# Block steps for two groups' queries and keys, adding transfers for weight sums, and down sums tied to half turns

## The chip, the core and the metric

The kernel runs on one core of a Trainium2 chip. The time is that of one execution on the device, in microseconds (us). The engines are named as in the profile: PE is TensorE (matmuls), PEld its loading of weights, DVE VectorE, ACT ScalarE, POOL GpSimd, and SP the engine that starts most transfers. A transfer that adds to its destination is started from POOL's queue (q0 in the profile); SP's and ACT's transfers are plain ones (q1).

## What is computed

One decoder layer on 512 tokens of width 1024, in float32: a half-step SwiGLU feed-forward part, a token mixer, and a second half-step feed-forward part, each with a norm ahead and behind.

```python
h = rms_norm(x, ffn1_pre);  x = x + 0.5 * rms_norm(swiglu(h, w_gate, w_up, w_down), ffn1_post)
h = rms_norm(x, mix_pre);   x = x + rms_norm(token_mixer(h, w_in, ...), mix_post)
h = rms_norm(x, ffn2_pre);  x = x + 0.5 * rms_norm(swiglu(h, ...), ffn2_post)

def token_mixer(h, w_in, ...):
    proj = h @ w_in                   # queries, keys, values of both attentions, gates
    o_nsa = nsa_attention(...)        # first attention: compressed, selected and window branch
    o_dil = dilated_attention(...)    # second: 3 groups of 4 heads, dilation 1, 4, 16
    y = sigmoid(g_a) * (o_nsa @ w_nsa_o) + sigmoid(g_b) * (o_dil @ w_dil_o)
    return y @ w_mix_out
```

## The kernel before

**Precision.** Each float32 operand is split into a rounded part and a remainder: a cast on ACT (line 153) and a subtraction on DVE (line 154). A product is three matmuls (`mm3`, lines 176 to 178): high by high, high by low, low by high. A weight tile of 128 x 1024 numbers is split into the pair `whi`, `wlo`, of which there are three buffers.

**Block products.** The feed-forward parts, and in the second attention half of the merge gates, use a form of matrix product in which a 2 x 2 arrangement of quarter products takes seven in place of eight. The quarters of the activation (first or second half of the width, first or second 256 tokens) are `B11`, `B21`, `B22`, and four sums of them are `T1` to `T4`. The matching weights are quarters (P1, P2, P4) or sums of quarters (P5, P6, P3, P7). Each of the seven steps is 24 matmuls with 256 columns. The token sums are made on DVE by `mix_token_sums`, kept split in slots named `SP`, `V` and `x`.

**The second attention** (`dil`). Three groups of four heads; a *turn* is a pair of heads, (group, pair). `project` makes a turn's queries and keys: two weight splits, two projections of 24 matmuls with 512 columns, then `q_parts` and `k_parts`, which scale, permute and split the result from PSUM into the slots `Q`, `KA`, `KB` (6 ACT and 4 DVE instructions of 64 x 512; POOL zeroes half of each `KB` tile). `attend` does the scores and softmax of the turn's two heads: matmuls into an `S` bank, a bias and row minimum on DVE (line 942), an exponential with row sum on ACT (line 943). Between the turns stand the *block steps*: `unit_blocks` yields the seven steps of a lot of gates, of which there are two, and `STEPS` says how many steps follow each turn. Their weight sums are made on DVE from raw quarters in SBUF (lines 1395 to 1401, four of 128 x 1024 for each lot). After the last turn the softmax statistics of the second and third group go through memory to be brought into token order (`sdram`, lines 1506 and 1552), the groups' weights are computed, POOL scales the stored probabilities with them (line 1583), and PE transposes these (lines 1630 and 1643). In between PE makes the values.

**The first attention** (`nsa`) goes over 16 heads and branches. Behind each, `sums(m)` starts transfers on POOL's queue: `table_sums` makes the sums of the down weights for the last feed-forward part, in four sets of up to three of its eleven row pairs (`b` = 0, 3, 6, 9), eight transfers for a set: four plain copies between tensors in memory and four that add. A set starts every third head.

**Order.** A scheduler lays out each engine's instructions when the kernel is built, by the order of the program and what is ready; a block `issue_after(i)` keeps instructions behind `i` on its engine. On the chip each engine and each queue goes through its list in order, and waits where an operand isn't there.

Of the kernel before, what the change touches and what calls it, by code (L numbers as in the profile page):

```python
# [12 lines left out]
F32 = mybir.dt.float32  # L13
# [4 lines left out]
OP = mybir.AluOpType  # L18
# [14 lines left out]
AHEAD = 2  # L33
STAGED = 5
STEPS = (3, 3, 1, 4, 2, 1)
# [20 lines left out]
GROUPS += [[(C_VD, 256)], [(C_VD + 256, 512)]] + [[(C_GA + u * P, 2 * P)] for u in range(0, 16, 2)]  # L56
PLACES = {}
# [17 lines left out]
class Layer:  # L75
# [1262 lines left out]
    def mix_token_sums(self, names):  # L1338
# [6 lines left out]
        def less(dst, a, t):  # L1345
            nc.vector.tensor_sub(dst, part(self.xht, *a), t)
            nc.vector.tensor_add(dst, dst, part(self.xlt, *a))

# [13 lines left out]
        if "T2" in names:  # L1362
            self.t2 = new()
            less(self.t2, (4, hi), self.t1)
            keep("T2", self.t2)
# [6 lines left out]
        if "T4" in names:  # L1372
            less(self.t2, (4, lo), self.t2)
            keep("T4", self.t2)

    def unit_loads(self, u):

        b = {}
        for h in range(2):
            r = self.pool.tile([P, 2, 4, 256], F32, name="raw", tag="raw", bufs=3)  # L1380
            for f in range(2):
                b[h, f] = r[:, f]
                self.nc.sync.dma_start(r[:, f], self.columns((C_GA + (u + 2 * f) * P, 2 * P))[:, 4 * h:4 * h + 4])
        return b

    def unit_blocks(self, u, b):

        nc = self.nc
        st = {}
        st["P5"], st["P6"] = [self.sbt("tmp", [P, 4, 256], bufs=2) for _ in range(2)]  # L1390

        def prep(name):
            with self.tc.issue_after(self.last_fold):
                if name == "P5":
                    nc.vector.tensor_add(st["P5"], b[0, 1], b[1, 1])
                if name == "P6":
                    nc.vector.tensor_sub(st["P6"], st["P5"], b[0, 0])
                if name == "P3":
                    nc.vector.tensor_sub(b[1, 0], b[1, 0], st["P6"])
                if name == "P7":  # L1400
                    nc.vector.tensor_sub(b[0, 1], b[0, 0], b[0, 1])
            src = dict(P1=b[0, 0], P2=b[1, 0], P7=b[0, 1], P4=b[1, 1], P3=b[1, 0]).get(name)
            st["w" + name] = self.wsplit(st[name] if src is None else src, [4, 256])

        def run(name):
            hi, lo = st["w" + name]
            key, top = dict(P1=("X", "B11"), P2=("Y", "B21"), P6=("X", "T2"), P5=("Z", "T1"), P7=("X", "T3"), P4=("X", "T4"),
                            P3=("Y", "B22"))[name]
            start = name in ("P1", "P2", "P5", "P3")
            if start:  # L1410
                st[key] = self.bank(dict(X="T", Y="V", Z="T")[key])
            for n in range(2):
                c = slice(n * P, (n + 1) * P)
                for j in range(4):
                    self.mm3(st[key][:, n * 256:(n + 1) * 256], hi[:, j, c], lo[:, j, c], self.tops[top][0](j),
                             self.tops[top][1](j), start and n == 0 and j == 0, False, True)

        def store(f, half, v):
            n = u + 2 * f
            nc.sync.dma_start(self.gdram[n:n + 2, :, 256 * half:256 * half + 256].rearrange("n p c -> p n c"),  # L1420
                              v.rearrange("p (n c) -> p n c", n=2))

        def finish(name):
            if name in ("P1", "P6", "P7", "P4"):
                v = st[name + "c"] = self.slot("ring")
                nc.scalar.copy(v, st["X"])
            for key in dict(P2="Y", P7="Z", P6="Z", P3="Y").get(name, ""):
                v = st[dict(P2="P1c", P7="P7c", P6="P6c", P3="P6c")[name]]
                nc.vector.tensor_add(v, st[key], v)
            if name in ("P2", "P7", "P4", "P3"):  # L1430
                store(*dict(P2=(0, 0), P7=(1, 1), P4=(1, 0), P3=(0, 1))[name], v)

        for name in ("P1", "P2", "P5", "P6", "P3", "P7", "P4"):
            prep(name)
            run(name)
            finish(name)
            yield

    def dil(self, fillers, early_gates):
# [16 lines left out]
        def project(g, j):  # L1456
            if j == 0:
                bias[g] = []
                for n in range(2 if g == 0 else 1):
                    w = self.slot("W")  # L1460
                    width = 256 if g == 0 else P
                    for m in range(S // width):
                        sl = -slopes[4 * g + 2 * n + m] * (1, 4, 4)[g]
                        o = w[:, m * width:(m + 1) * width]
                        nc.vector.tensor_scalar(o, (base0, self.dm[:, 384:512], base2)[g], sl, None, op0=OP.mult)
                        bias[g].append(o)
                stats.append(self.sbt(f"dst{g}", [P, NT, 4, 2]))
                probs.append([])
            b, _ = self.proj_T(raws[g, j][:, :, 0:P])
# [4 lines left out]
        def attend(g, j, q, kb, ka):  # L1474
            st = stats[g]
            for half in range(2):
# [28 lines left out]
            if j == 1 and g:  # L1505
                nc.sync.dma_start(self.sdram[g - 1].rearrange("(n r) c -> n r c", r=4), st.rearrange("p t h s -> p t (h s)"))
# [4 lines left out]
        lots = []  # L1511

        def blocks(n):
            for _ in range(n):
                if next(lots[0], 0) == 0:
                    lots.pop(0)
                    next(lots[0])

        def lot(u):
            lots.append(self.unit_blocks(u, self.unit_loads(u)))  # L1520
# [5 lines left out]
        for n, t in enumerate(turns):  # L1526
            pairs[t] = project(*t)
            if n == 0:
                lot(8)
                self.mix_token_sums(("T1",))  # L1530
            if n == 1:
                load(1, 0)
            if n == 2:
                self.mix_token_sums(("T2",))
                self.mix_token_sums(("T4",))
                self.mix_token_sums(("T3",))
            if n:
                attend(*turns[n - 1], *pairs.pop(turns[n - 1]))
                blocks(STEPS[n - 1])
            if n == 1:  # L1540
                load(1, 1)
            if n == 3:
                load(2, 0)
                lot(12)
                load(2, 1)
        attend(*turns[-1], *pairs.pop(turns[-1]))
        blocks(STEPS[-1])

# [161 lines left out]
    def mixer(self, post, finish, sums):  # L1710
# [21 lines left out]
        self.nsa(fill_half, sums)  # L1732
# [34 lines left out]
        self.dil(pieces(), lambda: [gate(d, 0, "KB") for d in range(EARLY)])  # L1767
# [155 lines left out]
    def run(self, out):  # L1923
# [10 lines left out]
        def boundary(post, pre, store, tags=None, shift=0):  # L1934
# [3 lines left out]
            def finish(t, gain):  # L1938
# [3 lines left out]
                if pre is not None:  # L1942
# [8 lines left out]
                   lambda m: [self.table_sums(a["d2"], td[1], b, m - b) for b in range(0, NP, 3)])  # L1951
# [51 lines left out]
```

## Time and profile before

| | us |
|---|---|
| median of 3 runs | 1110.22 (1108.45 to 1110.34) |
| the profiled execution | 1110.36 |
| its span | 1108.5 |
| PE busy | 1090.5 |
| DVE busy | 908.0 |
| ACT busy | 652.3 |
| POOL busy | 229.3 |

Busy time of PE covers the whole of a matmul, while the next one has begun already; the pace of the matmuls is read from their starts in the timeline. The stages that matter here, from the timeline: the first attention's heads run until about 517 us, the second attention's projections, scores and block steps from there to about 632, its values, transposes and outputs follow. A releaser in the profile is what an engine waited for last.

### The profile page before, as it was taken

What the parts mean: (1) busy time and instruction counts of PE and PEld (TensorE: products, weight loads), DVE (VectorE), ACT (ScalarE), POOL (GpSimd) and SP (SyncE); (2) the same over time, 40 slices, a digit from 0 to 9 for tenths busy, and PEclk for the clock granted to TensorE, in tenths of its full rate; (3) what the DMA queues carried; (4) which work ended last, traced back from release to release, by engine and by line L of the source; (5) the groups of instructions that cost most, each with busy time, mean ns of one, the idle gap of its engine ahead of it and who ended that gap; (6) DMA issues with size and microseconds to landing.
All of it is one profiled execution on the core that took longest, in us unless ns stands there. A gap on an engine that the chain in (4) does not pass through costs nothing.

```text
span 1108.5 us, 18921 instructions
## 1 busy us (share of the span) xinstructions
PE 1090.5 (98%) x7022; PEld 977.3 (88%) x7022; DVE 908.0 (82%) x1547; ACT 652.3 (59%) x1166; POOL 229.3 (21%) x312
## 2 busy tenths in 40 slices
PE   9999999999999999999999999999999999999997
PEld 7899999988789887777889998877989999998886
DVE  6989999998787988787977547876878999989575
ACT  7455555567565778675667636744435555567452
POOL 0444454310020056463000085001000000000001
PEclk9999999999999999999999999999999999999999
DMA  9899999999863498995231623573334444468862
GB/s 343 258 292 325 295 279 292 296 331 331 296 214 115 146 276 245 276 257 122 87 133 59 208 63 120 201 263 111 107 110 138 135 136 124 141 220 297 282 184 103
DMA packets 82652, 227.55 MB, mean 205 GB/s; under 512 B 12513, under 2 KB 17665, under 8 KB 79617
## 3 DMA queue, kind: packets, MB, share of 16 engines
q1 hardware_dynamic: 66192, 174.18, 46.3%
q0 software_dynamic: 16224, 51.91, 18.6%
q8 instruction: 55, 0.90, 0.3%
q14 instruction: 37, 0.30, 0.1%
q10 hardware_dynamic: 144, 0.26, 0.1%
HBM read 191.66 MB, written 57.72 MB: 225 GB/s over the span
## 4 chain that ended last, share of the span: by engine, by line
PE 69%; DVE 12%; ACT 7%; DMA 5%; POOL 3%; issue 3%; SPq 0%; DVEq 0%; POOLq 0%; ACTq 0%
PE pb_F L177 8%; PE pb_F L178 7%; PE pb_F L176 7%; PE pb_S L178 6%; PE pb_S L177 6%; PE pb_S L176 6%; PE pb_T L178 5%; PE pb_T L176 5%; PE pb_T L177 5%; DVE wlo L154 3%; DMA SP_s<-odram 2%; PE pb_V L177 2%; PE pb_V L178 2%; PE pb_V L176 2%; ACT whi L153 2%
## 5 line engine op out<-in xcount | busy, mean ns | idle before, releaser
L154 DVE TENSOR_TENSOR wlo<-raw,whi 128x1024 fp32r<-128x1024 f32 (+2 forms) x212 | 250.2, 1185 | 100.7 <-ACT whi L153 98.6
L153 ACT CAST whi<-raw 128x1024 fp32r<-128x1024 f32 (+2 forms) x212 | 215.3, 1019 | 149.8 <-PE pb_F L177 39.5
L176 PE MATMUL pb_F<-xhl_t,whi 128*128 128x512 f32 (+1 forms) x368 | 126.5, 344 | 0.4 <-DVE xhl_t L254 0.2
L178 PE MATMUL pb_F<-xhl_t,wlo 128*128 128x512 f32 (+1 forms) x368 | 125.6, 341 | 0.0
L177 PE MATMUL pb_F<-xhl_t,whi 128*128 128x512 f32 (+1 forms) x368 | 125.4, 341 | 0.0
L197 POOL TENSOR_TENSOR rs_t<-rs_t,mhalf_t 128x1 f32<-128x1 f32 x20 | 13.3, 666 | 465.4 <-DVE rs_t L193 465.4
L176 PE MATMUL pb_S<-xhl_t,whi 128*128 128x256 f32 (+1 forms) x280 | 83.3, 297 | 0.0
L177 PE MATMUL pb_S<-xhl_t,whi 128*128 128x256 f32 (+1 forms) x280 | 83.1, 297 | 0.0
L178 PE MATMUL pb_S<-xhl_t,wlo 128*128 128x256 f32 (+1 forms) x280 | 83.1, 297 | 0.0
L176 PEld LDWEIGHTS pb_F<-xhl_t,whi 128*128 128x128 f32 x368 | 69.2, 188 | 8.2 <-DVE xhl_t L254 0.9
L178 PEld LDWEIGHTS pb_F<-xhl_t,wlo 128*128 128x128 f32 x368 | 69.2, 188 | 7.5 <-DVE wlo L154 0.5
L177 PEld LDWEIGHTS pb_F<-xhl_t,whi 128*128 128x128 f32 x368 | 69.2, 188 | 6.8 <-issue 0.2
L153 ACT CAST whi<-tmp_t 128x1024 fp32r<-128x1024 f32 x40 | 40.6, 1051 | 37.0 <-DVE tmp_t L529 23.5
L1184 POOL TENSOR_SCALAR SP_s<-SP_s,st_t 128x384 f32<-128x384 f32 (+2 forms) x48 | 51.9, 1225 | 47.7 <-DVE st_t L1120 20.5
L177 PE MATMUL pb_T<-xhl_t,whi 128*128 128x256 f32 x216 | 59.9, 277 | 0.0
L176 PE MATMUL pb_T<-xhl_t,whi 128*128 128x256 f32 x216 | 59.9, 277 | 0.0
L178 PE MATMUL pb_T<-xhl_t,wlo 128*128 128x256 f32 x216 | 59.8, 277 | 0.0
L177 PEld LDWEIGHTS pb_S<-xhl_t,whi 128*128 128x128 f32 x280 | 52.6, 188 | 2.2
L176 PEld LDWEIGHTS pb_S<-xhl_t,whi 128*128 128x128 f32 x280 | 52.6, 188 | 2.2
L178 PEld LDWEIGHTS pb_S<-xhl_t,wlo 128*128 128x128 f32 x280 | 52.6, 188 | 2.2
L154 DVE TENSOR_TENSOR wlo<-tmp_t,whi 128x1024 fp32r<-128x1024 f32 x40 | 48.7, 1217 | 2.2 <-ACT whi L153 2.0
L176 PE MATMUL pb_T<-SP_s,whi 128*128 128x256 f32 x176 | 48.9, 278 | 0.0
(894 smaller groups left out, 3551.9 us busy)
## 6 DMA issues: line engine op xcount, KB each, us to landing
raw<-in_gu_dram SPq DMA_DIRECT2D x64, 512.0 KB, 4.8
raw<-tdram SPq DMA_DIRECT2D x40, 512.0 KB, 5.2
PT_s<-in_d_dram POOLq DMA_DIRECT2D x66, 256.0 KB, 6.7
raw<-in_d_dram SPq DMA_DIRECT2D x30, 512.0 KB, 4.5
raw<-in_w_in_dram SPq DMA_DIRECT2D x15, 1024.0 KB, 5.0
tdram<-in_d_dram POOLq DMA_DIRECT2D x18, 768.0 KB, 10.0
tdram<-PT_s POOLq DMA_DIRECT2D x44, 256.0 KB, 5.5
CP_s<-in_gu_dram SPq DMA_DIRECT2D x20, 512.0 KB, 4.2
```

The lines of the kernel that those rows point to most:

```text
L153: self.last_cast = self.nc.scalar.copy(dsthi, src).ins
L154: self.last_sub = self.nc.vector.tensor_sub(dstlo, src, dsthi.bitcast(F32)).ins
L176: mm(out, lhi, rhi, start=start, stop=False, skip_group_check=skip)
L177: mm(out, lhi, rlo, start=False, stop=False, skip_group_check=skip)
L178: self.last_mm = mm(out, llo, rhi, start=False, stop=stop, skip_group_check=skip).ins
L197: nc.gpsimd.tensor_tensor(out=r, in0=v, in1=self.mhalf, op=OP.pow)
L1184: self.last_pool = nc.gpsimd.tensor_scalar(pp, pp, st[:, 1, t:t + 1], None, op0=OP.mult).ins
```

## The change

- The queries and keys of groups 1 and 2 are no longer projected turn by turn. Each group's 512 columns are a lot of seven block steps, like the gates. The order of lots is group 1, first gates, group 2, second gates: 28 steps in all. `project` for these groups makes only biases and statistics.
- The joined results of a lot go through `token_rows`, which makes scaled, permuted and split queries and keys for 256 tokens at a time, two steps after the result.
- The weight sums P5, P6, P3 and P7 are made in memory: `lot_sums` starts plain and adding transfers on POOL's queue during the first attention, eight for each pair of lots, 1 MB each. A step's weight (or sum) is loaded whole, two at a time, and split two steps ahead.
- All four token sums are made behind the first turn's projection. `T2` and `T4` have the opposite sign, and so have the sums that use them.
- The turns are taken by halves: after each head's scores and softmax, `PLAN` says how many steps follow. Of the down sums of the last part, the first set stays in the first attention; the other three are started behind the half turns, each behind a POOL copy that waits for that half turn's statistics.
- The statistics' store is started from ACT's queue.

The core of the diff (loop heads and new helpers in part):

```diff
-STEPS = (3, 3, 1, 4, 2, 1)
+PLAN = (1, 2, 2, 5, 2, 2, 3, 5, 2, 1, 2, 1)
+LOTS = (0, 2, 1, 3)
+BLOCKS = ("P1", "P2", "P6", "P5", "P7", "P3", "P4")
...
+    def lot_sums(self, m, step):
+        put = self.nc.gpsimd.dma_start
+        s1, s2, s4, s3 = [v[:, 2 * m:2 * m + 2] for v in self.ldram]
...
+        if step == 0:
+            put(s1, part(1, 0))
+            put(s3, part(0, 0))
+        elif step == 1:
+            put(s2, part(0, 0))
+            put(s4, part(0, 1))
+        elif step == 3:
+            add(s1, part(1, 1))
+            add(s3, part(1, 0))
+        elif step == 6:
+            add(s2, s1)
+        elif step == 9:
+            add(s4, s2)
...
+    def load_blocks(self):
+        r = self.raw_tile([2, D])
+        for i in range(2):
+            self.nc.sync.dma_start(r[:, i], self.block_at(len(self.ready)))
+            self.ready.append(r[:, i].rearrange("p (k f) -> p k f", k=4))
...
+    def block_split(self, n):
+        while len(self.splits) <= min(n + SPLITS_AHEAD, 7 * len(LOTS) - 1):
+            m = len(self.splits)
+            self.splits.append(self.wsplit(self.ready[m], [4, 256]))
+            if m % 2 and len(self.ready) < 7 * len(LOTS):
+                self.load_blocks()
...
+            if name in ("P1", "P6"):
+                v = st[name] = place()
+                nc.scalar.copy(flat(v), src["X"])
+            elif name == "P5":
+                v = st["P6"]
+                nc.vector.tensor_sub(flat(v), flat(v), src["Z"])
+            elif name in ("P2", "P3"):
+                v = st["P1" if name == "P2" else "P6"]
+                nc.vector.tensor_add(flat(v), src["Y"], flat(v))
+                result(0, name == "P3", v, 1.0)
+            elif name == "P7":
+                v = place()
+                nc.scalar.mul(flat(v), src["X"], -1.0)
+                nc.vector.tensor_add(flat(v), src["Z"], flat(v))
+                result(1, 1, v, 1.0)
+            elif name == "P4":
+                result(1, 0, st["X"], -1.0)
...
+                for i in range(2):
+                    nc.scalar.mul(sel(q[i], rows[i]), qs[rows[i]], 0.125 * sign)
+                for i in range(2):
+                    nc.scalar.mul(sel(kz[i], rows[i]), ks[rows[i]], sign)
+                    nc.scalar.mul(sel(ka[i], rows[1 - i]), ks[rows[i]], sign)
...
+            return lambda *v: late.append((done[0] + 1 + 1, lambda: result(*v)))
...
-                nc.sync.dma_start(self.sdram[g - 1].rearrange("(n r) c -> n r c", r=4), st.rearrange("p t h s -> p t (h s)"))
+                nc.scalar.dma_start(self.sdram[g - 1].rearrange("(n r) c -> n r c", r=4), st.rearrange("p t h s -> p t (h s)"))
...
+        self.load_blocks()
+        for j in range(2):
+            pairs[0, j] = project(0, j)
+            self.load_blocks()
+            if j == 0:
+                for name in ("T1", "T2", "T4", "T3"):
+                    self.mix_token_sums((name,))
+        for i, n in enumerate(PLAN):
+            (g, j), half = turns[i // 2], i % 2
+            if (j, half) == (0, 0) and g:
+                project(g, 0)
+            attend(g, j, half)
+            mark = self.sbt("mark", [P, 1])
+            with self.tc.issue_after(nc.gpsimd.tensor_copy(mark, stats[g][:, 0, 2 * j + half, 0:1]).ins):
+                sums(i)
+            blocks(n)
...
+        def early_sums(m):
+            self.lot_sums(0, m)
+            self.lot_sums(1, m - 5)
+            sums(0, m - 2)
+
+        def late_sums(m):
+            for i in range(1, 4):
+                sums(3 * i, m - (0, 3, 5)[i - 1])
...
-                   lambda m: [self.table_sums(a["d2"], td[1], b, m - b) for b in range(0, NP, 3)])
+                   lambda b, step: self.table_sums(a["d2"], td[1], b, step))
```

More of the change, by code (lines that the diff above doesn't have):

```diff
@@ L1372, in mix_token_sums @@
         if "T4" in names:
-            less(self.t2, (4, lo), self.t2)
+            nc.vector.scalar_tensor_tensor(self.t2, self.t2, -1.0, part(self.xht, 4, lo), op0=OP.mult, op1=OP.subtract)
+            nc.vector.tensor_sub(self.t2, self.t2, part(self.xlt, 4, lo))
             keep("T4", self.t2)
[L1376 to L1384, printed above, removed]
@@ L1386, in unit_blocks, with lot_pair @@
-    def unit_blocks(self, u, b):
-        nc = self.nc
[L1389 to L1408, printed above, removed]
+    def lot_pair(self, m, f, h):
+        o = PLACES[[seg for seg in PLACES if seg[0] == LOT_AT[2 * m]][0]][0]
+        return self.a["w_in"][:, o:o + 8 * D].rearrange("p (l f h c) -> p l f h c", l=2, f=2, h=2)[:, :, f, h]
@@ new lines, in block_split, with lot_blocks, order, flat @@
+    def block_split(self, n):
[4 more added lines that the diff above has]
+                self.load_blocks()
+        return self.splits[n]
+    def lot_blocks(self, at, result):
+        nc = self.nc
+        lot = LOTS[at // 7]
+        st, keys = {}, dict(P1=("X", "B11"), P2=("Y", "B21"), P6=("X", "T2"), P5=("Z", "T1"), P7=("X", "T3"), P4=("X", "T4"),
+                            P3=("Y", "B22"))
+        tags = dict(X="F", Y="V", Z="F") if lot < 2 else dict(X="T", Y="V", Z="T")
+        home = []
+        if lot < 2:
+            for t in [self.sbt("tmp", [P, 2, S], bufs=2) for _ in range(2)]:
+                home += [t[:, 0], t[:, 1]]
+        def order(b):
+            return b.rearrange("p (m n r) -> p m r n", m=2, r=4) if lot < 2 else b
+        def flat(v):
+            return v.rearrange("p (m r n) -> p m r n", m=2, r=4) if lot < 2 else v
+        def place():
+            return home.pop(0) if home else self.slot("ring")
+        for n, name in enumerate(BLOCKS):
+            hi, lo = self.block_split(at + n)
+            key, top = keys[name]
@@ L1418, in store @@
[L1418 to L1436, printed above, removed]
+                    self.mm3(st[key][:, m * 256:(m + 1) * 256], hi[:, j, c], lo[:, j, c], self.tops[top][0](j),
+                             self.tops[top][1](j), start and m == 0 and j == 0, False, True)
+            src = {k: order(b) for k, b in st.items() if k in "XYZ"}
+            if name in ("P1", "P6"):
[15 more added lines that the diff above has]
+                result(1, 0, st["X"], -1.0)
@@ L1475, in attend, with gate_rows, result @@
+        def gate_rows(u):
+            def result(f, half, v, sign):
+                if sign < 0:
+                    b, v = v, self.slot("ring")
+                    nc.scalar.mul(v, b, sign)
+                n = u + 2 * f
+                nc.sync.dma_start(self.gdram[n:n + 2, :, 256 * half:256 * half + 256].rearrange("n p c -> p n c"),
+                                  v.rearrange("p (n c) -> p n c", n=2))
+            return result
+        def attend(g, j, half):
             st = stats[g]
-            for half in range(2):
+            q, kb, ka = pairs[g, j]
+            if half == 1:
+                del pairs[g, j]
+            for half in (half,):
@@ L1525, in dil @@
         load(0, 1)
[L1526 to L1547, printed above, removed]
+        self.ready, self.splits = [], []
+        self.load_blocks()
[14 more added lines that the diff above has]
+            blocks(n)
         nat = [stats[0]]
@@ L1730, in fill_half @@
                 fill(1)()
-        self.nsa(fill_half, sums)
+        NP = NF // 2
+        self.ldram = [tc.dram_tile([P, 4, D], F32, name=f"ldram{i}") for i in range(4)]
+        def early_sums(m):
[5 more added lines that the diff above has]
+                sums(3 * i, m - (0, 3, 5)[i - 1])
+        self.nsa(fill_half, early_sums)
         wn, wd = a["w_nsa_o"], a["w_dil_o"]
@@ L1765, in pieces @@
                         yield
-        self.dil(pieces(), lambda: [gate(d, 0, "KB") for d in range(EARLY)])
+        self.dil(pieces(), lambda: [gate(d, 0, "KB") for d in range(EARLY)], late_sums)
         behind = self.last_exp, self.last_cast
```

66 lines of the change are left out of this document (48 added, 18 removed).

## The prediction

> **What bounds the kernel now.** I read the page first, for the busy shares and the chain that ended last; then the table of windows over the second attention, where nearly every edit lies; then the timelines of TensorE and VectorE there, the view of the DMA queues, and the waits.
>
> ```profile
> span 1108.5 us, 18921 instructions
> PE 1090.5 (98%) x7022; PEld 977.3 (88%) x7022; DVE 908.0 (82%) x1547; ACT 652.3 (59%) x1166; POOL 229.3 (21%) x312
> PE 69%; DVE 12%; ACT 7%; DMA 5%; POOL 3%; issue 3%; SPq 0%; DVEq 0%; POOLq 0%; ACTq 0%
> ```
>
> ```profile
> 520.00:540.00 20.00, 19.39 (x93) 15.93 (x91) 19.76 (x26) 12.62 (x19) 0.52 (x1) 1.00 0.16 54
> 540.00:560.00 20.00, 20.00 (x126) 18.11 (x127) 19.58 (x35) 12.98 (x30) 0.52 (x1) 1.00 0.19 67
> 560.00:640.00 80.00, 79.95 (x545) 73.83 (x544) 51.09 (x129) 50.65 (x128) 3.12 (x6) 1.00 0.43 143
> 520.00:640.00 120.00, 119.34 (x760) 107.88 (x759) 90.44 (x189) 76.25 (x175) 4.17 (x8) 1.00 0.35 115
> ```
>
> The columns after the window are PE, PEld, DVE, ACT and POOL busy, the granted clock, the DMA share and GB/s. PE is full through the whole stage. Three things are seen beside it: DVE is full too from 520 to 560, POOL is almost idle (4 of 120 us), and the DMA engines are busy for a third (0.35). So a microsecond less of matmuls in this stage is a microsecond less of the kernel, as long as DVE, POOL and DMA, which the change loads, don't take PE's place.
>
> **What TensorE saves.** A busy PE hides the step between matmuls, so I take starts.
>
> ```profile
> 525.67 0.39 PE L177 MATMUL pb_F<-xhl_t,whi 128*128 128x512 f32 x1
> ...
> 531.34 0.39 PE L178 MATMUL pb_F<-xhl_t,wlo 128*128 128x512 f32 x1
> ...
> 537.34 0.28 PE L936 MATMUL pb_S<-KA_s,Q_s 128*128 128x256 f32 x1
> ...
> 542.87 0.28 PE L176 MATMUL pb_V<-xhl_t,whi 128*128 128x256 f32 x1
> ...
> 545.75 0.29 PE L176 MATMUL pb_T<-SP_s,whi 128*128 128x256 f32 x1
> ...
> 548.49 0.39 PE L176 MATMUL pb_F<-xhl_t,whi 128*128 128x512 f32 x1
> ...
> 629.71 0.27 PE L937 MATMUL pb_S<-KB_s,Q_s 128*128 128x128 f32 x1
> ```
>
> From 525.67 to 531.34 there are 25 steps of a 512-column matmul: 0.227 us each, so a projection of 24 takes 5.44 us. The two queries' and two keys' projections of a group take four: 21.8 us. In place of them stand seven blocks of 24 matmuls with 256 columns. A block whose moving operand is the activation itself takes 545.75 - 542.87 = 2.88 us, one with a sum kept in the SP slots 548.49 - 545.75 = 2.74 us. P1, P2 and P3 read the activation, and T3 lies in V and x slots, where I take the slower 2.88; P6, P5 and P4 take 2.74. Seven are 4 x 2.88 + 3 x 2.74 = 19.7 us. Each group saves 2.1 us, the two **4.1 us**. The 14 gate blocks, the scores (from 537.34, the last at 629.71) and the values are the same before and after.
>
> **What VectorE and ScalarE pay.** Here are the kinds of instruction that the edits add and remove.
>
> ```profile
> L154 DVE TENSOR_TENSOR wlo<-raw,whi 128x1024 fp32r<-128x1024 f32 x22 | 26.7, 1222 | 19.7 <-ACT whi L153 19.7
> ...
> L930 DVE SCALAR_TENSOR_TENSOR Q_s<-pb_F,Q_s 64x512 fp32r<-64x512 f32 x6 | 4.2, 694 | 0.1
> ...
> L1429 DVE TENSOR_TENSOR ring_s<-pb_T,ring_s 128x512 f32<-128x512 f32 x4 | 2.7, 685 | 0.9 <-ACT ring_s L1426 0.9
> L1395 DVE TENSOR_TENSOR tmp_t<-raw 128x1024 f32<-128x1024 f32 x2 | 2.4, 1222 | 2.1 <-DMA raw<-in_w_in_dram 2.1
> ...
> L1592 DVE TENSOR_TENSOR Q_s<-pb_F,Q_s 128x256 fp32r<-128x256 f32 x1 | 0.4, 416 | 0.0
> ```
>
> ```profile
> L153 ACT CAST whi<-raw 128x1024 fp32r<-128x1024 f32 x22 | 22.7, 1050 | 29.2 <-PE pb_F L177 25.1 <-PE pb_T L177 2.6 <-issue 1.2
> ...
> L1426 ACT COPY ring_s<-pb_T 128x512 f32<-128x512 f32 x8 | 4.7, 585 | 0.1
> ...
> L928 ACT ACTIVATE Q_s<-pb_F 64x512 fp32r<-64x512 f32 x6 | 3.6, 594 | 0.1
> ...
> L1591 ACT CAST Q_s<-pb_F 128x256 fp32r<-128x256 f32 x1 | 0.4, 368 | 0.0
> ```
>
> Splits go from 8 + 14 to 28: +6 x 1.22 on DVE, +6 x 1.05 on ACT. The eight weight sums of lines 1395 to 1401 leave DVE: -8 x 1.22. A pair's queries and keys took 6 ACT and 4 DVE instructions of 64x512; now each of two halves takes as many of 64x256. No row shows that shape; it lies between half of 0.69 (no gain or loss) and all of it (twice the cost). I take the 128x256 rows, 0.42 and 0.37, since duration goes by columns: DVE 32 x 0.42 - 16 x 0.69 = +2.4, ACT 48 x 0.37 - 24 x 0.59 = +3.6. Joining the products takes 16 DVE adds in place of 8 (+5.5) and 14 copies in place of 8 (+3.5). The sums: DVE +7.3 - 9.8 + 2.4 + 5.5 = **+5.4 us**, ACT 6.3 + 3.6 + 3.5 = **+13.4 us**. The last window holds 90.4 us of DVE and 76.3 of ACT in 120; with 96 and 90 in 116 neither is the bound on average, but the start is full already:
>
> ```profile
> 517.61 0.69 DVE L1217 TENSOR_TENSOR x_s<-pb_V,x_s 64x512 f32<-64x512 f32 x1 [1.66 <-ACT x_s L1216]
> ...
> 536.08 0.69 DVE L154 TENSOR_TENSOR SP_s<-CP_s,SP_s 128x512 fp32r<-128x512 f32 x1
> 536.69 1.22 DVE L1397 TENSOR_TENSOR tmp_t<-tmp_t,raw 128x1024 f32<-128x1024 f32 x1
> 537.83 1.22 DVE L1346 TENSOR_TENSOR CP_s<-xhl_t,CP_s 128x1024 f32<-128x1024 f32 x1
> ```
>
> From the last fold of the first attention (517.6 + 0.7 = 518.3 us) to the split that the tenth block needs, DVE has: the four token sums (10 passes at the 1.14 us between starts, 8 remainders at 0.61), 16.3; the first two pairs' parts and the second's splits (8 x 0.69 + 2 x 1.14), 7.8; ten block splits, 11.4; four half turns of softmax, four rows each at some 0.35, 5.5; joins, parts and biases of the first group, some 9. That is 50 us. PE is done with its projections at 537.34; four half turns of scores (about 0.95 each) and nine blocks are 29.4 us more, so it comes to the tenth block at 566.7: DVE has 48.4 us. Now the first 40 us of the stretch are as full (19.76 and 19.58 of 20) and cost PE almost nothing, because the token sums are spread past a second pair of projections, which the change takes out. Of a shortage of about 2 us I charge PE with **1.2 us**: zero if the joins of the last two blocks can wait, 2.4 if none can.
>
> **What DMA and the POOL queue pay.**
>
> ```profile
> q0 software_dynamic: 4608, 23.07, 64.6%
> q1 hardware_dynamic: 2581, 10.37, 21.0%
> ...
> raw<-in_w_in_dram SPq DMA_DIRECT2D x4, 1024.0 KB, 5.7
> raw<-in_w_in_dram SPq DMA_DIRECT2D x7, 512.0 KB, 9.1
> ...
> gdram<-ring_s SPq DMA_DIRECT2D x6, 256.0 KB, 7.5
> ```
>
> ```profile
> q1 hardware_dynamic: 6880, 13.72, 33.3%
> ...
> gdram<-ring_s SPq DMA_DIRECT2D x8, 256.0 KB, 2.3
> ```
>
> The first is the queues from 380 to 520 us (the first attention, which now carries all the down sums of the last part), the second from 520 to 645. The POOL transfers cost 0.646 x 140 / 23.07 = 3.9 us of all 16 engines per MB, SP's loads 0.21 x 140 / 10.37 = 2.8. The change swaps equal loads in the first attention: 16 transfers of 1 MB come, 24 of the 32 for the down sums go (16.8 MB either way), with only two after its eleventh head; I cost that at nothing. The 16.8 MB go to the second attention: 66 us of engines. Its weights grow as well, from 8.4 to 28 x 0.52 = 14.7 MB: +18 us on the 0.333 x 125 = 42 us of now. Together 126 us in a stage of about 120: **the DMA engines go from a third to full**. Who pays? Block weights are asked for about four blocks ahead, 11 to 15 us, and a load landed in 5.7 us (1 MB) or 9.1 (0.5 MB) beside the POOL transfers of the first attention; I charge nothing, the bound is a few microseconds in the two runs of five blocks. A late load would first hold its split, behind it on ACT and DVE the softmax rows and joins, and then PE.
>
> The POOL instructions that make adding transfers wait for earlier ones; behind them on POOL are the zeroing of key tiles, which comes free before the marks and has a whole turn to spare, and the scaling of the probabilities, which has none:
>
> ```profile
> 634.81 3.31 DMA sdram<-dst_t
> 638.19 1.82 DMA nat_t<-sdram
> ...
> 642.49 5.39 POOL PT_s L1583 x5
> ```
>
> ```profile
> 670.39 0.95 PE L1643 MATMUL pb_T<-ident_t,PT_s 128*128 128x128 f32 x7 [0.41 <-POOL CP_s L1583]
> ```
>
> In the chain, the last softmax statistics go through memory and back, POOL starts scaling at 642.5, and PE, with 40 us of other work after its last scores, arrives at the transposes 0.41 us too early, at 670.0. So any delay of that round trip is paid in full, as far as room isn't found. The change gives it some room: the last half turn's four rows stand alone after two blocks, where now eight rows run to 634.8, 5 us behind the scores at 629.7; half of them is about 2.4 us sooner. Against it stand two adding transfers, 1.3 MB or 5 us of engines, issued at that same half turn. I let the two cancel: **0 us**, bounds -0.4 (only the wait of now can go) and +8.0 (the rival below). Moving the statistics' store from SP's queue to ACT's costs one issue there and frees SP.
>
> The sum, on the profiled execution's own 1110.36 us (span 1108.5, 0.14 above the median): -4.1 + 1.2 + 0 = **-2.9 us, 1107.5**; against the median of 1110.22, 1107.3.
>
> **The rivals.**
>
> *The saving is eaten at the start.* DVE and ACT are in order, and PE has only two splits of lead (three weight buffers). For it: the two full windows, and the pair of projections that no longer covers the token sums. Against it: VectorE has 29 of 80 us free from 560 on. The whole shortage of 2.4 us, and 1 to 1.5 more in the runs of five blocks, where ACT has 15 us (5.3 of splits, 6.6 of parts, 3 of softmax and copies) to PE's 15: -4.1 + 2.4 + 1.3 = -0.4, **1109.8 us**. No measurable change; chance 0.25.
>
> *The statistics come home late.* The adds of the last turns wait for those two to three half turns earlier, and the DMA engines are full, so the transfers at the last half turn, and POOL behind them, slip; and the small store and load of the statistics share the engines with them. For it: a 256 KB store landed in 2.3 us on the quiet engines and in 7.5 beside the POOL transfers, 5.2 more; POOL has already waited for a transfer in this way, in the first attention, where PE's longest wait in all names VectorE:
>
> ```profile
> POOL tdram L1306 <- DMA tdram<-in_d_dram: 5.1, 1, 5.1
> ```
>
> ```profile
> PE pb_V L1208 <- DVE PT_s L154: 0.7, 2, 0.4
> ```
>
> Twice 5.2 on the round trip less 2.4 of room is +8.0. It decides from the point where the round trip, or POOL, is more than 2.4 us later than now. Against it: block loads end some 20 us before the end, which lets the engines catch up. With 8.0 and the -2.9 above: +5.1, **1115.3 us**; slower, chance 0.20. The Trainium skill, "DMA: Bandwidth & Descriptors", section "Queues, rings and completion order", says that a DMA engine serves its queue rows in turn and empties a whole packet from one before it switches. By that rule a store of many small rows waits behind one large packet at each turn, which speaks for this rival; the trace's 2.3 against 7.5 us agrees with it, but shows it only for rows of 2 KB.
>
> *The first attention gains too.* Only two POOL transfers are issued in its last five heads, where the wait of 5.1 us stands now. If 3 us of it reach PE today: -2.9 - 3 = -5.9, **1104.3 us**; chance 0.07. Against it: the 0.7 us above, and no PE wait there names POOL.
>
> **How the numbers follow.** The forecast has 0.48. A measurement of this kernel can tell about 0.2%, 2.2 us, from no change. Faster by more: 0.48 + 0.07 = 0.55; within: 0.25; slower by more: 0.20. The range reaches from 1103.8 (just below the third rival) to 1114.0: it takes in the first rival whole and the nearer half of the second's, and leaves out not quite 0.2.
>
> **What would show it.** TensorE should have 7 x 2 x 24 matmuls of 256 columns in place of 192 of 512, and the stage from 515 us to the last scores be about 3 us shorter. If VectorE is the cost, PE's waits between 550 and 570 us name the remainders of line 154 or the parts. If the statistics are, the wait ahead of the first transposes grows from 0.41 us, POOL's scaling starts more than 28 us before it, and the landing time of the statistics' store has grown from 3.3 us. Loads that land after their split is due would show as ACT's casts waiting for DMA. What would make me wrong altogether is a first attention that slows by its larger transfers (1 MB where now 768 KB), which I costed at nothing.

## The result, and the profile after

The changed kernel takes **1126.3 us** (median of 4 runs, 1125.4 to 1127.8) against 1110.3 us before in the same comparison: a ratio of 1.0149, with a 95% interval of 1.0131 to 1.0166. It is 16 us slower. The forecast was 1107.3 us and the range ended at 1114.0. The profiled execution took 1125.38 us.

The page of the changed kernel, span, busy time and the two large DMA queues:

```profile
span 1123.6 us, 19346 instructions
PE 1092.0 (97%) x7166; PEld 986.1 (88%) x7166; DVE 913.6 (81%) x1569; ACT 666.4 (59%) x1202; POOL 247.7 (22%) x340
...
q1 hardware_dynamic: 68208, 180.44, 47.0%
q0 software_dynamic: 20064, 68.69, 23.8%
```

TensorE's busy time grew by 1.5 us, DVE's by 5.6, and the engines that grew more are idle for much of the span: ACT by 14.1 us with 41% to spare, POOL by 18.4 with 78%. So the time looks like waiting, and the page can't say where. The table of windows over the second attention can (columns as before: PE, PEld, DVE, ACT, POOL, granted clock, DMA share, GB/s):

```profile
560.00:580.00 20.00, 18.64 (x159) 18.43 (x158) 16.68 (x39) 16.67 (x36) 3.88 (x9) 1.00 1.03 345
580.00:600.00 20.00, 20.00 (x172) 20.00 (x171) 13.64 (x38) 13.85 (x38) 6.20 (x12) 1.00 1.04 297
600.00:620.00 20.00, 12.17 (x80) 11.76 (x78) 3.23 (x5) 6.03 (x10) 1.67 (x2) 0.74 1.05 358
620.00:640.00 20.00, 14.98 (x111) 15.01 (x112) 15.87 (x37) 14.05 (x35) 2.84 (x5) 0.83 0.67 178
```

From 600 to 620 us every compute engine is slack at once: PE 12 of 20 us, DVE 3, ACT 6. Only the DMA share is full, at 1.05, and has been since 560 (a share of 1 or a little more is read as full here). TensorE's waits from 520 to 700 us, longest first (microseconds in total, times, longest):

```profile
PE pb_F L181 <- ACT tmp_t L1473: 6.7, 1, 6.7
PE pb_S L941 <- DVE KA_s L1542: 6.2, 1, 6.2
PE pb_T L181 <- ACT ring_s L1463: 1.4, 1, 1.4
```

Two waits make 12.9 us. The engines that they name are not to blame; their own rows say what they were waiting for. ScalarE's timeline in the stall (start, duration, and in brackets the idle time before it):

```profile
606.30 1.04 ACT L158 CAST whi<-raw 128x1024 fp32r<-128x1024 f32 x1 [6.99 <-DMA raw<-in_w_in_dram]
608.87 1.04 ACT L158 CAST whi<-raw 128x1024 fp32r<-128x1024 f32 x1 [1.52 <-DMA raw<-in_w_in_dram]
...
615.94 1.05 ACT L158 CAST whi<-raw 128x1024 fp32r<-128x1024 f32 x1 [5.53 <-DMA raw<-in_w_in_dram]
```

VectorE's timeline:

```profile
607.38 1.23 DVE L159 TENSOR_TENSOR wlo<-raw,whi 128x1024 fp32r<-128x1024 f32 x1 [8.52 <-ACT whi L158]
...
619.82 0.18 DVE L1638 TENSOR_TENSOR mn_t<-dst_t,nat_t 128x16 f32<-128x16 f32 x1 [8.05 <-DMA nat_t<-sdram]
619.91 0.68 DVE L1469 TENSOR_TENSOR tmp_t<-pb_V,tmp_t 128x512 f32<-128x512 f32 x1
```

ScalarE waits three times for a block weight, 14.0 us in all. VectorE waits behind it for the same weights, and then 8 us for group 1's statistics: the small minimum of line 1638 stands in its line ahead of the join of line 1469, and the key parts that PE wants come after that. The instructions of the block loads (line 1416) from 580 to 600 us show the source:

```profile
L1416 SPq DMA_DIRECT2D raw<-ldram x4: 320/380/2818, 579.7 to 597.4; - x4
...
L1416 SPq DMA_DIRECT2D raw<-in_w_in_dram x3: 328/346/423, 585.5 to 591.3; - x3
...
  ACT whi L158: 14.0, 3
...
DMA to landing us min/median/max: 8.7/20.9/25.4
```

The last line is the time from issue to landing: a load of 512 KB takes 20.9 us (median), 25.4 at most. By the prediction's count it is asked for 11 to 15 us ahead. In the trace of the kernel that has no sums in this stage (below), 10.4 to 19.2 us pass from the issue of a block load to the cast that needs it, for the loads issued from 560 to 605 us; this is called the lead. Late loads are the first suspect; the minimum on VectorE is a second, and the block steps themselves a third.

### The profile page after: what moved, and what is told of

The parts are those of the page before. It is cut to its first block, busy times and chain, and to the rows that moved or that the text cites. A ratio compares the mean times of both kernels' runs of the same rounds, so it can differ in the third digit from the quotient of the medians.

```text
span 1123.6 us, 19346 instructions
## 1 busy us (share of the span) xinstructions
PE 1092.0 (97%) x7166; PEld 986.1 (88%) x7166; DVE 913.6 (81%) x1569; ACT 666.4 (59%) x1202; POOL 247.7 (22%) x340
## 4 chain that ended last, share of the span: by engine, by line
PE 64%; DVE 15%; DMA 8%; ACT 7%; issue 3%; POOL 2%; SPq 0%; DVEq 0%; POOLq 0%; ACTq 0%
PE pb_S L183 7%; PE pb_S L182 7%; PE pb_S L181 6%; PE pb_F L183 6%; PE pb_F L182 6%; PE pb_F L181 6%; PE pb_T L183 4%; PE pb_T L181 4%; PE pb_T L182 4%; DVE wlo L159 4%; PE pb_V L181 2%; PE pb_V L182 2%; PE pb_V L183 2%; ACT whi L158 2%; DMA gdram<-ring_s 2%
## 5 line engine op out<-in xcount | busy, mean ns | idle before, releaser
L159 DVE TENSOR_TENSOR wlo<-raw,whi 128x1024 fp32r<-128x1024 f32 (+2 forms) x222 | 262.8, 1188 | 98.2 <-ACT whi L158 94.7
L158 ACT CAST whi<-raw 128x1024 fp32r<-128x1024 f32 (+2 forms) x222 | 226.1, 1020 | 139.5 <-PE pb_F L183 19.8
L202 POOL TENSOR_TENSOR rs_t<-rs_t,mhalf_t 128x1 f32<-128x1 f32 x20 | 13.3, 664 | 455.9 <-DVE rs_t L198 455.9
L181 PE MATMUL pb_F<-xhl_t,whi 128*128 128x256 f32 (+1 forms) x320 | 106.3, 332 | 0.4 <-DVE KA_s L926 0.2
L183 PE MATMUL pb_F<-xhl_t,wlo 128*128 128x256 f32 (+1 forms) x320 | 105.3, 329 | 0.0
L182 PE MATMUL pb_F<-xhl_t,whi 128*128 128x256 f32 (+1 forms) x320 | 105.0, 328 | 0.0
L181 PEld LDWEIGHTS pb_F<-xhl_t,whi 128*128 128x128 f32 x320 | 60.3, 188 | 5.8 <-issue 0.9
L183 PEld LDWEIGHTS pb_F<-xhl_t,wlo 128*128 128x128 f32 x320 | 60.2, 188 | 5.1 <-DVE wlo L159 0.5
L182 PEld LDWEIGHTS pb_F<-xhl_t,whi 128*128 128x128 f32 x320 | 60.3, 188 | 4.3 <-issue 0.2
L1189 POOL TENSOR_SCALAR SP_s<-SP_s,st_t 128x384 f32<-128x384 f32 (+2 forms) x48 | 49.0, 1051 | 50.5 <-DVE st_t L1125 20.2
L158 ACT CAST whi<-tmp_t 128x1024 fp32r<-128x1024 f32 x36 | 36.4, 1052 | 30.4 <-DVE tmp_t L534 23.5
L183 PE MATMUL pb_T<-SP_s,wlo 128*128 128x256 f32 x176 | 48.8, 277 | 0.0
```

The costliest lines, as they stand in the source:

```text
L158: self.last_cast = self.nc.scalar.copy(dsthi, src).ins
L159: self.last_sub = self.nc.vector.tensor_sub(dstlo, src, dsthi.bitcast(F32)).ins
L181: mm(out, lhi, rhi, start=start, stop=False, skip_group_check=skip)
L182: mm(out, lhi, rlo, start=False, stop=False, skip_group_check=skip)
L183: self.last_mm = mm(out, llo, rhi, start=False, stop=stop, skip_group_check=skip).ins
L202: nc.gpsimd.tensor_tensor(out=r, in0=v, in1=self.mhalf, op=OP.pow)
```

## The experiments

Theories at the start: **A**, full DMA engines make both the block weights and the statistics late, and both cost PE; **B**, only the order costs (VectorE's minimum ahead of the joins); **C**, late block weights alone; **D**, too much ScalarE and VectorE work in the runs of five blocks.

**Sums later, and the statistics moved.** Four kernels. The first issues the late sums after the last scaling on POOL:

```diff
-            mark = self.sbt("mark", [P, 1])
-            with self.tc.issue_after(nc.gpsimd.tensor_copy(mark, stats[g][:, 0, 2 * j + half, 0:1]).ins):
-                sums(i)
             blocks(n)
...
+        with self.tc.issue_after(scaled):
+            for i in range(len(PLAN)):
+                sums(i)
```

> All steps of the three late sets of down sums are issued after the last scaling on POOL, none at a half turn; everything else is as changed (1126.3 us). Theory A (16.8 MB of adding transfers fill the DMA engines at 560 to 620 us; block loads and group 1's statistics come late): the 16.2 + 3.8 us that PE loses between 600 and 640, and most of 3.2 + 2.5 us beside it, go: 1103 to 1107 us, ACT's casts wait under 1 us for loads. Rival B (the order alone: VectorE's minimum over group 1's statistics stands ahead of the joins and parts): a quiet round trip still costs some 4 us ahead of the joins, 1108 to 1112 us. Rival D (too much ACT and DVE work in runs of five blocks): the stall stays, 1120 us or more. If the transfers hurt the merge stage behind, that shows as new PE waits after 700 us.

The second leaves the sums and moves the statistics (the third kernel does both, the fourth has only the lines of `mn`):

```diff
+            with self.tc.issue_after(self.last_load):
                 nc.sync.dma_start(n_.rearrange("p t h s -> p t (h s)"), self.sdram[g].rearrange("(t p) c -> p t c", p=P))
...
+        with self.tc.issue_after(self.last_soft):
             nc.vector.tensor_tensor(mn, nat[0][:, :, :, 0], nat[1][:, :, :, 0], op=OP.min)
```

> The sums stay at the half turns; the two loads of statistics stand behind the last block load on SP's queue, and VectorE's first minimum behind the last softmax. Theory A: the wait of 6.2 us for DVE and what the lower clock adds to it go, the wait of 6.7 us for late loads stays: about 1116 to 1120 us. Rival B: both waits go, 1106 to 1110 us. Rival C (late loads alone; the minimum only waits in a gap that the loads make anyway): 1123 to 1126 us.

> Both edits. Theory A: within 2 us of the run with the sums later alone, 1102 to 1107 us, since a quiet round trip costs little. Rival B: 3 us or more below that run.

> Only VectorE's first minimum stands behind the last softmax; the loads of statistics stay where they are on SP's queue, ahead of two block loads. If VectorE's place in line is what the statistics cost, this is within 1 us of the run that moves both. If SP's queue is (a load of statistics that waits for its store holds block loads behind it), it stays near 1126 us and the other run is lower.

Measured: sums later **1144.2 us** (ratio 1.0314, 1.0299 to 1.0330), statistics behind **1125.9** (1.0146, 1.0129 to 1.0163), both 1142.4 (1.0297, 1.0281 to 1.0312), minimum alone 1127.4 (1.0162, 1.0146 to 1.0177). No theory had expected the first; its expectation named only the sign, new waits after 700 us. Its windows say why:

```profile
600.00:620.00 20.00, 19.29 (x164) 19.12 (x164) 15.37 (x31) 17.30 (x36) 0.00 (x0) 1.00 0.51 172
...
700.00:720.00 20.00, 11.34 (x51) 9.16 (x50) 7.94 (x17) 5.21 (x10) 3.94 (x7) 0.82 1.02 327
720.00:740.00 20.00, 14.82 (x50) 11.12 (x49) 8.07 (x13) 5.75 (x9) 3.33 (x4) 0.84 1.03 320
740.00:760.00 20.00, 4.06 (x9) 2.79 (x10) 5.93 (x9) 6.45 (x10) 2.45 (x3) 0.59 1.06 252
```

The second attention is whole again: PE 19.29 of 20 us where it had 12.17, at a DMA share of 0.51. The first transposes start at 668.9 us, 1.5 before those of the kernel before (670.39). But the same 16.8 MB, let loose at once, fill the engines from 685 to 770 us, and PE stalls there instead, by more. The stall has gone where the sums went: that rules out D, whose ACT and DVE work is all still in place.

Moving the statistics does what it says and buys nothing. TensorE's waits of that kernel:

```profile
PE pb_F L181 <- ACT tmp_t L1473: 7.2, 1, 7.2
PE pb_S L941 <- DVE KA_s L1542: 2.5, 1, 2.5
PE pb_S L181 <- ACT whi L158: 2.4, 1, 2.4
```

The wait for the key parts falls from 6.2 to 2.5 us and the last scores come 4.7 us sooner (640.1 against 644.8). But then PE waits for the value weights (the third row), and the first transposes start at 687.15 us, as in the changed kernel (687.04). So B falls as it stood: group 1's minimum is a wait in the shadow of others. A's price for this run, 1116 to 1120 us, was missed as well; 1125.9 us lies where C had put it. The run with the minimum alone can't be told from this one (their intervals overlap), nor the run with both edits from the one with the sums later. What holds the value weights is left open here and taken up by the last two runs.

**How many bytes it takes.** The sums are moved to where the engines are free: one step with each pair of the last part, some 17 us apart.

```diff
             if opened:
                 sums_behind(ev[:, 0:1], p + 1)
+            else:
+                mark = self.sbt("mark", [P, 1])
+                with self.tc.issue_after(nc.gpsimd.tensor_copy(mark, x[:, 0:1]).ins):
+                    for i in rest:
+                        self.table_sums(wd, td, 3 * i, p - (0, 0, 1)[i - 1])
```

`rest` is (1, 2, 3) with none left at the half turns, (2, 3) or (3,) with one or two sets left there. These and the fourth keep the statistics behind, so that they compare with 1125.9 us for all three sets. The fourth has all three at the half turns, with `accum_op` set to bypass: it leaves out the additions of these sets and moves the same bytes.

> As the run with the statistics behind, but the three late sets of down sums are issued one step at a time with the pairs of the last part (some 17 us apart, from 790 us on, where the DMA share is 0.3 to 0.5 without them). Theory C (the DMA engines are full at 560 to 620 us, block loads land later than they are asked ahead, nothing else): second attention as in the run with both edits, first transposes 2 us sooner than before; 66 us of engines spread over some 140 us of the last part give a share of 0.8 to 0.9 there, no new wait: 1107 to 1109 us. Rival (adding transfers on POOL's queue slow whatever runs beside them): new waits of PE in the last part, 1112 us or more.

> One of the three late sets stays at the half turns, two go to the last part. Theory C with a threshold: 22 us of engines more in the second attention leave the share under 0.9, block loads land in under 11 us, which is the least that they are asked ahead; within 1.5 us of the run with none at the half turns. Rival (each MB moved costs its share of the 18 us): 5 to 7 us above that run.

> Two of the late sets at the half turns, one in the last part. Threshold: 44 us of engines more, share near 1 in the run of five blocks at 590 to 605 us, loads land in 10 to 16 us: 2 to 8 us above the run with none. In proportion: 11 to 13 us above it.

> All three late sets at the half turns, with plain transfers of the same bytes in place of the adding ones: the additions of three of the four sets of down sums are left out. If it is the bytes that fill the engines: the stall stays, within 3 us of 1126 us. If adding is what is dear (its transfers hold an engine longer per byte): 1112 to 1120 us, with a DMA share at 560 to 620 well under 1.

The sets are not of one size: the first two that are left at the half turns have three row pairs each (6.3 MB), the third has two (4.2 MB). The shares are those of the windows, the landings those of the block loads issued from 580 to 600 us (median and longest):

| sets at the half turns | median us | ratio to before, 95% | DMA share 560:580, 580:600, 600:620 | landing us |
|---|---|---|---|---|
| 0 | 1107.9 | 0.9972 (0.9961 to 0.9983) | 0.54, 0.65, 0.51 | 4.4, 5.4 |
| 1 | 1108.0 | 0.9973 (0.9962 to 0.9985) | 0.88, 0.87, 0.63 | 5.8, 9.4 |
| 2 | 1113.7 | 1.0030 (1.0016 to 1.0043) | 1.03, 1.04, 0.79 | 14.7, 17.9 |
| 3 | 1125.9 | 1.0146 (1.0129 to 1.0163) | 1.03, 1.04, 1.04 | 23.2, 25.7 |
| 3, plain transfers | 1113.3 | 1.0022 (1.0012 to 1.0032) | 0.98, 1.00, 0.76 | 15.0, 18.7 |

This is a threshold, not a price by the byte. The first set, some 25 us of engines at the prediction's 3.9 us per MB, costs nothing (the landing stays under the lead), the second, of the same size, costs 5.7 us, and the third, the smallest, some 12. (The row of all three was measured in another comparison than the others; by the ratios it lies 19 us above the run with none, by the medians 18.) Time is lost once landings reach the lead, which is 10.4 to 19.2 us here. (The run with two sets spreads from 1110.5 to 1117.8 us and its trace is of the longest, so its landings may be longer than usual.) The sets also start at different half turns, so their number and their place are not told apart. The plain transfers cost as much as two adding sets: adding is dear. My expectation for that run, with a low share, was right in the time and wrong in the share. What adding costs can be read from the POOL queue's rows of the two runs, of all three sets adding (span 1124.8 us) and of the plain ones (span 1111.1):

```profile
q0 software_dynamic: 20064, 68.69, 23.8%
```

```profile
q0 software_dynamic: 20064, 68.69, 22.4%
```

The bytes are the same, the engine time 268 and 249 us. Half of the three sets' transfers, 8.4 MB, were adding ones: an estimate of 2.2 us of all engines per MB on top of a plain transfer. Full engines are not what makes the difference, since the adding sets took as long when they were spread over the last part (24.7% of 1106.1 us, 273 us).

**Each part alone.** Two kernels: the kernel before with the sums tied to its half turns and nothing else (`marked` issues a mark and the sums' step for each of a turn's two halves), and the changed kernel with the sums moved to the pairs and nothing else (the edit above, `rest` of all three sets).

```diff
             if n:
                 attend(*turns[n - 1], *pairs.pop(turns[n - 1]))
+                marked(n - 1)
...
-        self.nsa(fill_half, sums)
+        self.nsa(fill_half, lambda m: sums(0, m - 2))
```

> The kernel before with one part of the change alone: the three late sets of down sums are tied to its half turns, all projections, gate blocks and statistics stay as they were. 66 us of engines come to the 42 of now in a stage of about 120 us. Theory C: the stage's own loads are few (8.4 MB), but their lead is as short; the engines are full in the middle of the stage and PE waits there for splits: 1114 to 1122 us. If the stall needs the larger weights of the block steps (14.7 MB): 1110 to 1112 us.

> The changed kernel with one edit: the three late sets go with the pairs of the last part, the order of the statistics is as changed. Theory C: as the run that also moved the statistics, 1107 to 1109 us, and the wait of VectorE for group 1's statistics is under 1 us. If the order of the statistics has a price of its own on quiet engines: 1 to 4 us above that run.

The sums alone: **1125.4 us**, ratio 1.0133 (1.0114 to 1.0152). The rest of the change alone: **1108.5 us**, ratio 0.9983 (0.9972 to 0.9994). One part carries nearly the whole loss, in a stage of 8.4 MB of weights as in one of 14.7; I had expected 1114 to 1122 us of it. The two effects add up to 1.0116 against the 1.0149 of the whole change, so some 3.7 us may come only where both parts meet; that is little more than the intervals allow. What it delays differs, however. The chain of waits of the kernel with the sums alone, and VectorE's longest wait for a DMA there:

```profile
639.88 16.60 DMA sdram<-dst_t
656.54 1.87 DMA nat_t<-sdram
```

```profile
DVE mn_t L1566 <- DMA nat_t<-sdram: 16.1, 1, 16.1
```

Here the store of the last statistics, 16 KB, lands after 16.6 us; before it took 3.3. (In the changed kernel, which starts it from ACT's queue, it takes 10.4 us; how much of the 16.6 is the full engines and how much the loads ahead of it in SP's queue is not shown.) The last scores come only 5.1 us later than before (634.8), the first transposes 14.6 (684.9): most is lost behind the scores. In the changed kernel block weights are asked for all through the stage, and they are late first.

With the sums in the last part alone, the block loads of 580 to 600 us (line 1421 in that kernel) land in time:

```profile
DMA to landing us min/median/max: 3.8/4.7/5.1
```

And the last part takes the 16.8 MB without a trace on PE. The window is 790 to 990 us, first of the kernel before, then of this one:

```profile
790.00:990.00 200.00, 200.00 (x1659) 195.34 (x1658) 181.32 (x226) 107.20 (x148) 0.00 (x0) 1.00 0.43 132
```

```profile
790.00:990.00 200.00, 200.00 (x1655) 195.33 (x1654) 180.94 (x228) 108.30 (x150) 26.23 (x34) 1.00 0.73 220
```

The DMA share rises from 0.43 to 0.73 and PE stays at 200.00 of 200 (I had expected 0.8 to 0.9 over some 140 us). Both versions with the sums there beat the kernel before, by 2 to 3 us; which of them is better (1107.9 with the statistics moved, 1108.5 without) these runs can't tell, as the intervals overlap. VectorE waits 1.2 us for group 1's statistics in the second, a little more than the 1 us that I had named.

**How late statistics reach PE.** ScalarE's timeline of the kernel with the sums alone, after the last scores:

```profile
658.86 0.42 ACT L1572 ACTIVATE fac_t<-fac_t 128x16 f32<-128x16 f32 x3 [17.32 <-DVE fac_t L1571]
...
659.70 1.05 ACT L153 CAST whi<-raw 128x1024 fp32r<-128x1024 f32 x1
```

ScalarE stands 17.3 us ahead of the exponential of the merge factors, which needs the statistics, and the casts of the value weights stand behind it. So in two kernels the factors' instructions were put behind the copies of the first group's values, on both engines:

```diff
-        mn = self.sbt("mn", [P, NT, 4])
...
-        nc.vector.reciprocal(z, z)
...
         kept = self.kept
+        with self.tc.issue_after(kept[0]), self.tc.issue_after(kept[1]):
+            mn = self.sbt("mn", [P, NT, 4])
...
+            nc.vector.reciprocal(z, z)
```

> As the run with the statistics behind (1125.9 us, all sums at the half turns), but the merge factors' minima, exponentials and reciprocal stand behind the copies of the first group's values on VectorE and ScalarE. In that run ScalarE stood 14.3 us ahead of the first exponential of the factors with the casts of two value weights behind it, and PE waited 2.4 + 1.3 + 1.0 us for those and ran at a lower clock. If the home-coming statistics hold the value weights in this way: 4 to 7 us less, 1119 to 1122 us. If the value weights themselves land late: no change, 1125 to 1127 us. If POOL's scaling, which starts later, then ends last: 1125 us or more, with a wait for POOL ahead of the first transposes well over 0.5 us.

> The kernel with the sums alone (1125.4 us) with the same edit. There ScalarE stood 17.3 us ahead of that exponential, and PE waited 5.4 + 0.8 us for value weights and lost some 3 us to the clock. If the statistics hold the value weights: 7 to 10 us less, 1115 to 1119 us. If the weights land late themselves: 1124 to 1127 us. POOL as in the other run.

Measured: **1122.4 us** (1.0109, 1.0092 to 1.0126) with the blocks, against 1125.9 without the edit, and **1119.7** (1.0083, 1.0068 to 1.0098) with the sums alone, against 1125.4. The waits for value weights are gone in both, so it was the statistics that held them, by way of ScalarE's line: 3.6 us in the one kernel, 5.7 in the other, both a little less than I had expected (4 to 7 and 7 to 10). In the second the transposes of the next groups then wait for POOL, which starts late:

```profile
PE pb_T L1640 <- POOL x_s L1615: 2.4, 2, 1.4
```

TensorE's timeline shows the two waits:

```profile
673.30 0.96 PE L1653 MATMUL pb_T<-ident_t,PT_s 128*128 128x128 f32 x7 [0.64 <-DVE V_s L1571]
...
678.44 0.33 PE L1640 MATMUL pb_T<-ident_t,x_s 128*128 128x128 f32 x1 [1.42 <-POOL x_s L1615]
...
679.75 1.64 PE L1640 MATMUL pb_T<-ident_t,x_s 128*128 128x128 f32 x3 [0.98 <-POOL x_s L1615]
...
688.06 0.93 PE L1653 MATMUL pb_T<-ident_t,PT_s 128*128 128x128 f32 x7
```

The first transposes come only 2.9 us later than before. The next batch over `PT_s` comes 9.1 us later (688.06 against 678.97), about the 9.2 us that this kernel still loses: behind the waits for POOL the granted clock was 0.50 from 680 to 685 us. So with ScalarE's line freed, the late statistics cost some 6 us through POOL.

With the blocks the two waits at 600 to 640 us remain, 6.9 and 3.8 us, both behind late block weights. So C alone is not enough, and A holds, with its parts in another order than I thought: block weights first, then the last statistics, and group 1's statistics hardly. (No run puts the values first and leaves group 1's minimum where it was, so what the minimum would cost then is open.)

## Why the prediction was wrong, step by step

- **TensorE saves 4.1 us, VectorE at the start takes 1.2 back**: borne out as a sum. Without the sums at the half turns the forecast of 1107.3 us (0.9974 of before) lies within both intervals. The stage from the last fold of the first attention to the last scores is 112.1 us before and 110.1 and 110.6 in these two kernels: 2.0 and 1.6 us shorter, where I had named about 3. How the sum splits into its two terms was not measured, so some of the agreement may be luck. Of the term for VectorE, PE's steps from 560 to 580 us took 2.5 us more than its matmuls at full pace (from 0.227 us for 512 columns), against 0.8 before: 1.7 more, in the bounds of 0 to 2.4. The cause was off: the largest wait there, 1.4 us, is for ScalarE's copy out of the T bank (line 1463), not for a remainder on VectorE.
- **VectorE +5.4, ScalarE +13.4 us**: measured +5.6 and +14.1, and harmless.
- **"The DMA engines go from a third to full"**: right, 1.03 to 1.05 from 560 to 620 us (0.79 over 520 to 640).
- **"I charge nothing, the bound is a few microseconds in the two runs of five blocks"**: this is the step that failed. I set a lead of 11 to 15 us against landings of 5.7 and 9.1 us, and those rows came from the first attention, whose engines were at 0.86. At a full share those landings no longer held: they went to 20.9 us (median), and 14.0 us of ScalarE's time passed in waiting for three weights. The charge of the sums at the half turns is 18 us (1125.9 of all sets less 1107.9 of none); 3.6 of them went when the values no longer stood behind the statistics, so some 14 us are left for the late weights and the slow clock behind the waits. I had written down the 126 us of transfers in a stage of 120 and then priced the transfers as if they fitted. The sign that I named for it, ScalarE's casts waiting for DMA, is what the trace shows. That each late weight would be followed by joins and parts, and those by PE, was right as well.
- **The statistics, 0 us, and the rival of 1115.3 us**: the rival had the right cause, full engines, and its mechanism is real, but not the largest here (3.6 us). Its price for the round trip was too small: with the sums alone the store took 13.3 us more, not 5.2. And its way was another at first: I led it through POOL, reading the 0.41 us ahead of the first transposes as a sign that any delay there is paid in full. It is none. The same wait, 0.35 us, stands there in the changed kernel and in the one with the values first, though POOL starts scaling 22.1 and 17.7 us ahead of the transposes there, and 27.9 before: POOL had 10 us to spare. What had none was ScalarE's line, where the exponentials stand ahead of the value weights. Past those 10 us the path through POOL does cost: with the sums alone and the values first POOL starts 12.3 us ahead, and PE waits for it.
- **The first attention, nothing in either direction**: right. From 380 to 520 us its DMA share is 0.86, as the two queues' 85.6% before, and PE's steps in the kernel with the sums in the last part show the same excess there as before.

The stall of the changed kernel from 600 to 640 us adds up as follows: 6.7 us of wait for ScalarE, 6.2 for VectorE, and 4.4 us by which the steps behind each ran slow (5.3 us for 24 steps that take 2.9, then 4.4 for 21 that take 2.4). TensorE's timeline around the first wait:

```profile
603.48 0.28 PE L183 MATMUL pb_V<-xhl_t,wlo 128*128 128x256 f32 x1
610.46 0.58 PE L181 MATMUL pb_F<-SP_s,whi 128*128 128x256 f32 x1 [6.70 <-ACT tmp_t L1473]
610.84 0.41 PE L182 MATMUL pb_F<-SP_s,whi 128*128 128x256 f32 x1
611.05 0.41 PE L183 MATMUL pb_F<-SP_s,wlo 128*128 128x256 f32 x1
...
615.95 0.28 PE L182 MATMUL pb_T<-xhl_t,whi 128*128 128x256 f32 x1
616.07 0.28 PE L183 MATMUL pb_T<-xhl_t,wlo 128*128 128x256 f32 x1
```

## What to carry to other kernels

Add up the transfers of a stage before you price any one of them: below a full share the loads here landed within their lead (9.4 us at most at 0.88), and at a full one the lead of 10.4 to 19.2 us was not enough (20.9 us, median). Whether a longer lead would have been, no run shows. Work that nobody waits for yet, such as tables for a later part, belongs where the engines have room, and paced: released at once, the same bytes cost some 36 us in one place (1144.2 us against 1108.5) and, spread, nothing that PE shows in another. A wait that names an engine is a question to that engine's own rows; here both named engines were waiting for DMA.

## What the runs showed of the hardware that was not expected

A wait of 6.7 us cost more than its length. Steps of a 256-column matmul went from 0.12 us ahead of it to 0.21 behind it; the granted clock from 610.46 to 615.75 us was 0.50:

```profile
610.46:615.75 5.29, 5.29 (x25) 5.29 (x26) 1.31 (x2) 0.00 (x0) 0.00 (x0) 0.50 1.05 311
```

The same happened after the wait of 6.2 us, until 629.4; the wait of 1.4 us at 560 to 580 left the clock at 1.00. (Two waits close together, of 1.4 and 1.0 us, were followed by 0.50 from 680 to 685 us in the kernel with the sums alone and the values first.) The Trainium skill, "TensorE: Matmul & The Clock Gate", section "Part 1: The HAM clock gate", says that the clock falls to half after an idle window of about 3.4 us and comes back after a busy one of the same length. The traces agree on the half; they show 5.4 and 4.4 us until it is back.

Two more. An adding transfer took an estimated 2.2 us of all 16 engines per MB more than a plain one of the same bytes (268 against 249 us for 8.4 MB of additions). And a store of 16 KB took 16.6 us from SP's queue and 10.4 from ACT's beside full engines, where it took 3.3 us before: a small transfer was not spared.
